# A decoder trunk in fp32: how the first branch's operands get their norm, and how the norm's reciprocal roots are stored

## The chip, the cores and the metric

The kernel runs on 1 core of a Trainium2 chip. The metric is the device time of one execution in microseconds (us). The engines are PE (matrix products and transposes; PEld is its weight load, which overlaps), DVE, ACT and POOL (element work), and SP, which here issues nearly all transfers. Each engine and SP's queue take their instructions strictly in the order in which the program lists them; an instruction that waits holds all behind it on that engine.

## The reference

One layer of a decoder trunk, with x of [1, 1024, 1024] in fp32. One input projection feeds three token mixers; their outputs are gated, summed, projected and added to x; an MLP follows. Branch A, the first, is differential attention with 4 heads of value width 128, and it ends in a norm over each head's 128 values, a gain (`subln`) and the branch's own projection:

```
w   = p[0] - lam * p[1]                      # two softmaxes of one head
o_A = einsum('bhqk,bhke->bqhe', w, v)        # 4 heads x 128 values per token
y_A = o_A * rsqrt(mean(o_A * o_A, -1) + EPS) * subln   (times a constant)
y_B = sliding-window attention (8 heads); y_C = sparse attention (8 heads)
x  <- x + W_o(sum over n of sigmoid(G_n) * (y_n @ P_n))
x  <- x + W_down relu(W_up RMSNorm(x))^2
```

## The kernel before, in words

**Precision.** Each fp32 matrix is split into a rounded part and a remainder, `hi` and `lo`. `split` (L86 to L91) does this with an ACT copy (L90) and a subtraction on DVE or POOL (L91), and `mm3` (L113 to L120) makes one product from three matmuls (L118, L119, L120). `weight` (L93 to L103) loads a weight tile into a box `wr` (L100, queue SP), ACT copies it to `wh` (L90), POOL subtracts to `wl` (L91). There are 4 boxes `wr` in the attention of branch A, 2 in that of branch C.

**Stages.** Projection of head 0 (to about 90 us); compression of keys (to 130); branch A, four heads, each beside the projections of the next head (130 to 446); branch B (to 580); branch C in two groups (580 to 860 and 860 to 1200); merge (to 1300); MLP (to 2058). While attention runs in small steps on PE (scores L714, transposes of probabilities L762, value products L894 and L895), `mix` (L167) fills PE with dense work: projections, later gate products (`gates`), and in the second group of branch C the first branch's own projection, `first_branch` (L1148).

**Order.** PE's order is the program's order, set by `mix` from estimated costs. On the other engines and on SP's queue the framework's scheduler sets the order when the kernel is built; it is fixed thereafter. `step` (L698) runs a list `late` of closures a counted number of steps after they are put there.

**A head's end.** For each block `qb` of 256 queries, `values` stores the raw head output `o` to DRAM (`od`, L867). Three steps later `norms` (L875 to L883) sums its squares on PE (L878), and DVE makes the mean plus EPS times the softmax's denominators (L880) in a small tile `sso` of 128 x 2; POOL raises that to -0.5 (L881); SP stores it to `rd` (L883). The store turns columns into a row, so that it consists of 256 elements of 4 bytes, 1 KB in all; there are 16 such stores, 4 in each head. Around the turn from one head to the next the same queue carries the projection's weights (`wr<-wa`, `wr<-wb`) and, once in each of the first three turns, `spread_bias` (L393 to L398): one DRAM-to-DRAM copy `bd<-bs` of 768 KB, issued behind the last of a group of weight loads.

**The first branch.** `first_branch` works in two halves of 512 tokens. In each it runs gate products, and in the midst of them, at their steps 3, 7, 11 and 15, it calls `operand` (L1120) for the heads 0 to 3: load 128 x 512 of `od` into a box `wr` (L1123), which it shares with the weights; load the reciprocal roots of 256 tokens, repeated over 128 partitions, into a box `y` (L1128), twice; multiply both on DVE (L1130), 128 x 256 each, by `subln` and the roots; then `split` into `xh` (ACT) and `xl` (DVE). Then the branch's 8 products follow. `merge_and_mlp` calls `operand` without roots.

**Boxes.** The boxes `tm` (2 of 128 x 1024 floats) serve `project` (a projection's normed queries and keys, which PE transposes at L561) and, in `first_branch`, the gates `g` that the 8 products use.

Of the kernel before, what the change touches and what calls it, by code (L numbers as in the profile page):

```python
# [11 lines left out]
F32 = mybir.dt.float32  # L12
F32R = mybir.dt.float32r
AF = mybir.ActivationFunctionType
ALU = mybir.AluOpType
AX = mybir.AxisListType

P = 128
# [57 lines left out]
class Kernel:  # L76
# [27 lines left out]
    def parts(self, pool=None, bufs=None, tag="w"):  # L104
        pool = pool or self.wp
        if self.other is not None:
            self.turn += 1
            pool = self.other if self.turn % 2 else pool
        return [pool.tile([P, self.w_n], F32R, name=tag + x, tag=tag + x, bufs=bufs or self.w_bufs) for x in "hl"]
# [225 lines left out]
    def constants(self, tmp):  # L335
        nc, a, c = self.nc, self.a, self.ca
        ld = nc.sync.dma_start

        gains = tmp.tile([P, 8, HD], F32, name="gains")
        ld(gains, a["qk_gain"].broadcast_to([P, 8, HD]))  # L340
        stt = nc.vector.scalar_tensor_tensor
        stt(self.gk[:, 0, :], gains[:, 0, :], -0.125, gains[:, 1, :], op0=ALU.mult, op1=ALU.mult)
        stt(self.gk[:, 1, :], gains[:, 2, :], -0.125, gains[:, 3, :], op0=ALU.mult, op1=ALU.mult)
        stt(self.gk[:, 2, :], gains[:, 4, :], -0.125, gains[:, 5, :], op0=ALU.mult, op1=ALU.mult)
        stt(self.gsw[:, 0, :], gains[:, 4, :], -0.125, gains[:, 6, :], op0=ALU.mult, op1=ALU.mult)
        stt(self.gsw[:, 1, :], gains[:, 4, :], -0.125, gains[:, 7, :], op0=ALU.mult, op1=ALU.mult)

        dl = tmp.tile([P, 4, HD], F32, name="dl")
        ld(dl, a["diff_lambda"].broadcast_to([P, 4, HD]))
        pr = tmp.tile([P, 2, HD], F32, name="pr")  # L350
        nc.vector.tensor_tensor(pr, dl[:, 0:4:2, :], dl[:, 1:4:2, :], op=ALU.mult)
        ls = tmp.tile([P, 4], F32, name="ls")
        nc.vector.tensor_reduce(ls[:, 0:2], pr, axis=AX.X, op=ALU.add)
        nc.scalar.activation(ls[:, 2:4], ls[:, 0:2], AF.Exp)
        self.nlam = c.tile([P, 1], F32, name="nlam")
        stt(self.nlam, ls[:, 3:4], -LAM_INIT, ls[:, 2:3], op0=ALU.add, op1=ALU.subtract)
        self.subln = c.tile([P, 1], F32, name="subln")
        ld(self.subln, a["diff_subln"])
        nc.vector.tensor_scalar(self.subln, self.subln, 1.0 - LAM_INIT, None, op0=ALU.mult)
        self.sink = c.tile([P, 2, 8], F32, name="sink")  # L360
        ld(self.sink[:, 0, :], a["sinks"].broadcast_to([P, 8]))
        nc.vector.tensor_scalar(self.sink[:, 1, :], self.sink[:, 0, :], -1.0, None, op0=ALU.mult)
        self.wmask = c.tile([P, P], F32, name="wmask")
        ld(self.wmask, a["c_wmask"])
        self.cval = c.tile([P, 1], F32, name="cval")
        ld(self.cval, a["c_cval"])
        self.pos = c.tile([P, 2, 16], F32, name="pos")
        ld(self.pos, a["cmp_pos"])
        self.cgate = c.tile([P, NT, 24], F32, name="cgate")

        c.tile([P, 56], F32, name="gap2")
        self.kct = c.tile([P, 2, P], F32R, name="kct")
        self.vct = c.tile([P, 2, P], F32R, name="vct")
        nc.gpsimd.memset(self.vct[64:P].bitcast(F32), 0.0)
# [417 lines left out]
    def items_a(self, h, sta):  # L792
        nc, at = self.nc, self.at
        bias = self.bias[:, h, :]
        for qb in range(4):
            pq = [None, None]
            box = {}
# [48 lines left out]
            rows = []  # L846
            for j in range(2):
                t = 2 * qb + j
# [26 lines left out]
            def norms(box=box, qb=qb):  # L875
                pt = self.tr()
                for j in range(2):
                    nc.tensor.matmul(pt[:, j:j + 1], box["o2"][:, j * P:(j + 1) * P], self.ones, start=True, stop=True)  # L878
                ss = at.tile([P, 2], F32, name="sso", tag="sso", bufs=2)
                nc.vector.scalar_tensor_tensor(ss, pt[:, 0:2], 1.0 / P, box["eps"], op0=ALU.mult, op1=ALU.add)  # L880
                nc.gpsimd.tensor_tensor(ss, ss, self.nhalf[:, 0:2], op=ALU.pow)  # L881
                r = self.rd[h]
                nc.sync.dma_start(bass.AP(tensor=r.tensor, offset=r.offset + qb * 256, ap=[[1, P], [P, 2]]), ss)  # L883

            yield dict(rows=rows, groups=groups, end=[norms])

# [230 lines left out]
                nc.sync.dma_start(self.gd[f, :, hs], o)  # L1117


    def operand(self, src, s, hi, lo, rows=None):  # L1120

        raw = self.wp.tile([P, 512], F32, name="wr", tag="wr", bufs=self.wr_bufs)
        self.nc.sync.dma_start(raw, src[:, s])  # L1123
        if rows is not None:
            for o in (0, 256):
                r = self.sq.tile([P, 256], F32, name="y", tag="y", bufs=2)
                src = bass.AP(tensor=rows.tensor, offset=rows.offset + s.start + o, ap=[[0, P], [1, 256]])
                self.nc.sync.dma_start(r, src)  # L1128
                v = raw[:, o:o + 256]
                self.nc.vector.scalar_tensor_tensor(v, v, self.subln, r, op0=ALU.mult, op1=ALU.mult)  # L1130
        self.split(hi, lo, raw)


    def gate(self, pool, tag, bufs, n, d, s):
        nc = self.nc
        g = pool.tile([P, 512], F32, name="g", tag=tag, bufs=bufs)
        nc.sync.dma_start(g, self.gd[n * KT + d, :, s])
        return g
# [9 lines left out]
    def first_branch(self):  # L1148
        nc = self.nc
        for half, n, m in ((0, GATES[3], GATES[4]), (1, GATES[5], 24 - sum(GATES))):  # L1150
            s = slice(half * 512, half * 512 + 512)
            yield from self.gates(n)
            o = [self.parts(tag="x") for _ in range(4)]
            for k, c in enumerate(self.gates(m)):
                if k % 4 == 3 and k // 4 < 4:
                    self.operand(self.od[k // 4], s, *o[k // 4], self.rd[k // 4])
                yield c
            for d in range(KT):
                w = self.weight(self.a["wbr"][0, d], 512)
                g = self.gate(self.sq, "tm", 2, 0, d, s)  # L1160
                ps = self.branch(0, d, [x[0] for x in o], [x[1] for x in o], w)
                with self.tc.high_priority(offset=self.urgent):
                    nc.vector.scalar_tensor_tensor(g, g, 1.0, ps, op0=ALU.add, op1=ALU.mult)
                nc.sync.dma_start(self.yd[d, :, s], g)
                yield 2.6
# [424 lines left out]
```

## Time and profile before

| | |
|---|---|
| median of 3 runs | 2058.51 us (2051.08 to 2060.27) |
| the profiled execution | 2060.21 us, its span 2058.4 us |
| mean clock granted to PE over the span | 0.971 of full |
| matrix engine's weight loads (PEld) | 1630.0 us busy, 79% of the span |
| queue SP in all (q1) | 213.87 MB, 32.7% of 16 transfer engines |
| stage of branch A, 180 to 446 us | PE idle 34 us of 266 |

How to read the rows that follow. A row of the timeline has the start, the duration, the engine, the line, the operation, output and inputs, and in square brackets the idle time of that engine just before and what released it; SPq is SP's queue, where a duration is that of the issue and not of the transfer. A row of transfers has the count, the size of each, and the median time from issue to landing. A row of windows has the stretch, its length, and for PE, PEld, DVE, ACT and POOL the busy time (with the instructions), then the clock granted to PE (1 is full), the share of time the transfer engines were busy, and GB/s. A row of groups has the count, the busy time and the mean nanoseconds of one, and the idle time before them with what ended it. In a row of waits stand the sum, the times and the longest, in us.

### The profile page before, as it was taken

Reading aid. Unit: us, or ns where it says so; the run is one execution under the profiler, and the core shown is the slowest. Engines: PE = TensorE matmul, PEld = TensorE weight load, DVE = VectorE, ACT = ScalarE, POOL = GpSimd, SP = SyncE. Lnnn points to the kernel's source line nnn. Section 1 sums busy time; section 2 is a strip of 40 time slices with the busy share of each in tenths; the row PEclk is TensorE's granted clock in tenths of the full one; section 3 lists DMA queues with packets and bytes.
Section 4 is the critical chain, followed back from the end, with each engine's and each line's share of the span. In section 5 each row is a group of like instructions: output and inputs, shape, how many; then the busy total and the mean of one; then the engine's idle time right before and its main releaser. Section 6 shows DMA issues by size and latency. Waiting matters only on the chain. (4 is left out here: it accounts for less than half of the span.)

```text
span 2058.4 us, 30688 instructions
## 1 busy us (share of the span) xinstructions
PE 1905.6 (93%) x9838; PEld 1630.0 (79%) x9838; DVE 1417.6 (69%) x3232; ACT 1005.4 (49%) x2546; POOL 951.4 (46%) x1142
## 2 busy tenths in 40 slices
PE   7998988989899999998998888999799998999988
PEld 7888878878688888887887677788688886888876
DVE  6756766778848677647677745747755444889898
ACT  5455545556636555535555533325455544444331
POOL 4455445544362212161221327217554445789783
PEclk9999999999999999999999999999999999999998
DMA  5132022211211111203142546424544446345343
GB/s 217 51 103 55 10 54 53 31 31 37 85 29 60 61 47 56 73 32 110 60 133 86 182 173 201 163 91 156 176 165 163 143 149 245 118 165 163 123 143 113
DMA packets 129214, 221.60 MB, mean 108 GB/s; under 512 B 19028, under 2 KB 42068, under 8 KB 129052
## 3 DMA queue, kind: packets, MB, share of 16 engines
q1 hardware_dynamic: 127468, 213.87, 32.7%
q10 hardware_dynamic: 1584, 5.77, 0.8%
q8 instruction: 78, 1.28, 0.3%
q14 instruction: 84, 0.69, 0.1%
HBM read 158.68 MB, written 64.83 MB: 109 GB/s over the span
## 5 line engine op out<-in xcount | busy, mean ns | idle before, releaser
L91 POOL TENSOR_TENSOR wl<-wr,wh 128x512 fp32r<-128x512 f32 (+3 forms) x246 | 328.5, 1341 | 303.2 <-ACT wh L90 260.0
L90 ACT ACTIVATE wh<-wr 128x512 fp32r<-128x512 f32 (+3 forms) x258 | 150.2, 590 | 210.2 <-PE mm L119 113.7
L714 PE MATMUL sc<-st 128*128 128x256 f32 (+5 forms) x736 | 185.9, 347 | 29.4 <-ACT p L746 29.0
L90 ACT ACTIVATE ph<-tr 128x384 fp32r<-128x384 f32 (+3 forms) x280 | 138.6, 498 | 111.3 <-PE tr L762 88.8
L91 DVE TENSOR_TENSOR pl<-tr,ph 128x384 fp32r<-128x384 f32 (+3 forms) x280 | 155.5, 559 | 48.7 <-ACT ph L90 46.7
L759 POOL MEMSET ph<- 128x128 f32 x152 | 34.6, 227 | 298.3 <-PE ac L894 245.8
L714 PEld LDWEIGHTS sc<-st 128*128 128x128 f32 x736 | 125.0, 196 | 50.8 <-ACT p L746 41.8
L118 PE MATMUL mm<-hh,wh 128*128 128x512 f32 x384 | 161.6, 421 | 0.0
L762 PE MATMUL tr<-ident,p 128*128 128x128 f32 x792 | 132.8, 281 | 27.7 <-DVE st L567 23.6
L119 PE MATMUL mm<-hl,wh 128*128 128x512 f32 x384 | 154.3, 402 | 0.0
L120 PE MATMUL mm<-hh,wl 128*128 128x512 f32 x384 | 153.9, 401 | 0.0
L119 PE MATMUL mm<-wl,wh 128*128 128x512 f32 x352 | 140.5, 399 | 9.5 <-POOL wl L91 9.5
L118 PE MATMUL mm<-wh 128*128 128x512 f32 x352 | 140.4, 399 | 8.3 <-DVE x L1472 5.4
L90 ACT ACTIVATE wh<-u 128x512 fp32r<-128x512 f32 x162 | 93.0, 620 | 108.0 <-PE mm L119 29.4
L120 PE MATMUL mm<-wh,wl 128*128 128x512 f32 x352 | 139.6, 397 | 0.0
L746 ACT ACTIVATE p<-sc,mc 128x256 f32<-128x256 f32 (+5 forms) x200 | 106.8, 539 | 52.7 <-DVE mc L738 48.4
L894 PE MATMUL ac<-ph,st 128*128 128x256 f32 x392 | 111.1, 301 | 19.1 <-DVE ob L901 9.8
L91 POOL TENSOR_TENSOR wl<-s,wh 128x512 fp32r<-128x512 f32 x64 | 89.1, 1400 | 77.8 <-ACT wh L90 77.8
L762 PEld LDWEIGHTS tr<-ident,p 128*128 128x128 f32 x792 | 95.7, 145 | 29.6 <-DVE st L567 24.9
L118 PE MATMUL mm<-wh,hh 128*128 128x384 f32 (+1 forms) x320 | 118.0, 369 | 0.6 <-ACT raw L523 0.6
L91 DVE TENSOR_TENSOR wl<-u,wh 128x512 fp32r<-128x512 f32 x98 | 112.0, 1145 | 4.0 <-ACT wh L90 4.0
L895 PE MATMUL ac<-pl,st 128*128 128x256 f32 x392 | 107.0, 293 | 7.3 <-DVE pl L91 6.7
(307 smaller groups left out, 5744.0 us busy)
## 6 DMA issues: line engine op xcount, KB each, us to landing
ud<-u SPq DMA_DIRECT2D x112, 256.0 KB, 2.1
u<-ud SPq DMA_DIRECT2D x98, 256.0 KB, 3.4
wr<-wu SPq DMA_DIRECT2D x76, 256.0 KB, 2.8
wr<-wd SPq DMA_DIRECT2D x64, 256.0 KB, 3.0
gd<-go SPq DMA_DIRECT2D x48, 256.0 KB, 2.0
g<-gd SPq DMA_DIRECT2D x48, 256.0 KB, 3.1
wr<-wg SPq DMA_DIRECT2D x40, 256.0 KB, 2.8
wr<-wbr SPq DMA_DIRECT2D x40, 256.0 KB, 2.9
```

Of the source, the lines that this page charges most:

```text
L90: nc.scalar.activation(hi, src, AF.Copy)
L91: (eng or nc.vector).tensor_tensor(lo, src, hi.bitcast(F32), op=ALU.subtract)
L118: mm(out, lh, rh, start=first, stop=False, skip_group_check=more)
L119: mm(out, lh, rl, start=False, stop=False, skip_group_check=more)
L120: mm(out, ll, rh, start=False, stop=last, skip_group_check=more)
L714: self.nc.tensor.matmul(ps[:, off:off + k1 - k0], q[:, t * P:(t + 1) * P], k[:, k0:k1], start=i == 0, stop=i == 1)
L746: self.nc.scalar.activation(p, ps, AF.Exp, bias=m, scale=-1.0, accum_out=l)
L759: nc.gpsimd.memset(ph[0:rows, o:o + P].bitcast(F32), 0.0)
L762: nc.tensor.transpose(pt[0:rows, o:o + P], src, self.ident)
L894: nc.tensor.matmul(ac, v, ph, start=first, stop=False)
L895: nc.tensor.matmul(ac, v, pl, start=False, stop=last)
```

## The change

**The roots.** DVE writes the sums of all four blocks of a head into one tile `rms` of 128 x 8 on chip. Only after the fourth does POOL raise all 8 columns to -0.5, in one instruction, and three steps later `rows_of_head` transposes them on PE to 8 x 128, ACT copies them to `rr`, and SP stores them to `rd` as 8 rows of 512 bytes.

**The operands.** `scaled` takes the place of `operand` in `first_branch`. A box `tm` holds 512 columns of the raw head output in its first half and the repeated roots of the same 512 tokens in its second (two loads). When the step comes, POOL multiplies the one by the other, ACT makes `xh` with `subln` as its scale, DVE makes `xl` in one instruction. The loads for heads 0 and 1 are listed ahead of the gate products, those of heads 2 and 3 once the parts of heads 0 and 1 are listed. These operands no longer use boxes `wr` or `y`.

```diff
-        c.tile([P, 56], F32, name="gap2")
+        self.rms = c.tile([P, 4, 8], F32, name="rms")
+        c.tile([P, 24], F32, name="gap2")
...
-                ss = at.tile([P, 2], F32, name="sso", tag="sso", bufs=2)
+                ss = self.rms[:, h, 2 * qb:2 * qb + 2]
                 nc.vector.scalar_tensor_tensor(ss, pt[:, 0:2], 1.0 / P, box["eps"], op0=ALU.mult, op1=ALU.add)
-                nc.gpsimd.tensor_tensor(ss, ss, self.nhalf[:, 0:2], op=ALU.pow)
-                r = self.rd[h]
-                nc.sync.dma_start(bass.AP(tensor=r.tensor, offset=r.offset + qb * 256, ap=[[1, P], [P, 2]]), ss)
+                if qb == 3:
+                    r = self.rms[:, h, :]
+                    nc.gpsimd.tensor_tensor(r, r, self.nhalf, op=ALU.pow)
+                    self.late.append([3, rows_of_head])
+
+            def rows_of_head():
+                pt = self.tr()
+                nc.tensor.transpose(pt[0:8, 0:P], self.rms[:, h, :], self.ident)
+                r = at.tile([8, P], F32, name="rr", tag="sso", bufs=1)
+                nc.scalar.activation(r, pt[0:8, 0:P], AF.Copy)
+                nc.sync.dma_start(self.rd[h].rearrange("(t j) -> t j", j=P), r)
...
+    def scaled(self, i, s, hi, lo):
+        nc = self.nc
+        box = self.sq.tile([P, self.tm_n], F32, name="tm", tag="tm", bufs=2)
+        raw, r = box[:, 0:512], box[:, 512:1024]
+        row = self.rd[i]
+        nc.sync.dma_start(raw, self.od[i, :, s])
+        nc.sync.dma_start(r, bass.AP(tensor=row.tensor, offset=row.offset + s.start, ap=[[0, P], [1, 512]]))
+
+        def parts():
+            nc.gpsimd.tensor_tensor(raw, raw, r, op=ALU.mult)
+            nc.scalar.activation(hi, raw, AF.Copy, scale=self.subln)
+            nc.vector.scalar_tensor_tensor(lo, raw, self.subln, hi.bitcast(F32), op0=ALU.mult, op1=ALU.subtract)
+
+        return parts
...
+            parts = [self.scaled(i, s, *o[i]) for i in range(2)]
             for k, c in enumerate(self.gates(m)):
-                if k % 4 == 3 and k // 4 < 4:
-                    self.operand(self.od[k // 4], s, *o[k // 4], self.rd[k // 4])
+                if k % 4 == 3 and parts:
+                    parts.pop(0)()
+                    if k < 8:
+                        parts.append(self.scaled(2 + k // 4, s, *o[2 + k // 4]))
                 yield c
```

**Order on SP's queue, second head turn.** Before, the weight loads of the next projection (`wr<-wa`, `wr<-wb`) and the roots' stores (`rd<-sso`) stand so:

```order
L867 DMA od<-o_3041 128x256
L100 DMA wr<-wa 128x384
L883 DMA rd<-sso 128x2x1
L100 DMA wr<-wa 128x384 x3
L398 DMA bd_782<-bs 128x4x384
L100 DMA wr<-wb 128x396 x3
```

Now, with `rd<-rr` for the 8 rows of a head:

```order
L868 DMA od<-o_3031 128x256
L100 DMA wr<-wa 128x384 x4
L399 DMA bd_783<-bs 128x4x384
L100 DMA wr<-wb 128x396 x4
L868 DMA od<-o_3245 128x256
L892 DMA rd<-rr 8x128
```

The store from between the weight loads is gone; the head's one store stands behind all of them. The other turns change alike; at the third turn one `wr<-wb` stands right behind an `rd<-rr`.

**Order on SP's queue, first half of the first branch.** Before, where the operands' loads (`wr<-od`, `y<-rd`) follow four gate weights:

```order
L100 DMA wr<-wg 128x512 x4
L1123 DMA wr<-od 128x512
L1128 DMA y<-rd 128x256 x2
L1123 DMA wr<-od 128x512
L1117 DMA gd<-go 128x512
L1128 DMA y<-rd 128x256 x2
```

Now, at the same place:

```order
L100 DMA wr<-wg 128x512 x6
L1126 DMA gd<-go 128x512
L100 DMA wr<-wg 128x512
L1141 DMA tm<-od 128x512
L1142 DMA tm<-rd 128x512
L1126 DMA gd<-go 128x512
L100 DMA wr<-wg 128x512
L1141 DMA tm<-od 128x512
```

The gate weights come ahead of the operands' loads. The box of the first waits for the last projection's use of it; the third and fourth wait for the parts of heads 0 and 1.

**Order on ACT, second half of the first branch.** Before, the four `xh` copies stand among the exponentials (`p`, `pc`) and the copies of transposed probabilities (`ph`):

```order
L1116 ACTIVATE go<-mm 128x512
L90 ACTIVATE xh<-wr 128x512
L746 ACTIVATE pc_7154,lc<-sc,mc 128x64
L90 ACTIVATE ph<-tr 128x384
L90 ACTIVATE xh<-wr 128x512
L746 ACTIVATE p,lc<-sc,mc 128x448
```

Now they stand some 20 rows earlier in the order and are released by POOL's product:

```order
L747 ACTIVATE pc_7131,lc<-sc,mc 128x64
L1146 ACTIVATE xh<-tm,subln 128x512
L90 ACTIVATE ph<-tr 128x512
L747 ACTIVATE p,lc<-sc,mc 128x256
L90 ACTIVATE ph<-tr 128x384
L747 ACTIVATE p,lc<-sc,mc 128x256
```

A copy that waits still holds the exponentials behind it; what it waits for is another engine and other loads.

## The prediction and its working, on record before the run

> **What bounds the kernel now.** The page first. PE is busy nearly all the time, so what can be won is time in which PE waits or is slow.
>
> ```profile
> span 2058.4 us, 30688 instructions
> PE 1905.6 (93%) x9838; PEld 1630.0 (79%) x9838; DVE 1417.6 (69%) x3232; ACT 1005.4 (49%) x2546; POOL 951.4 (46%) x1142
> ```
>
> The change touches two places, branch A (the roots' stores) and the first branch inside branch C (the operands). For branch A, the waits of PE from 150 to 450 us, then PE's own rows after its four longest waits:
>
> ```profile
> PE tr L762 <- DVE st L567: 23.6, 7, 6.8
> ...
> 198.97 1.12 PE L762 MATMUL tr<-ident,p 128*128 128x128 f32 x4 [3.89 <-DVE pl L91]
> ...
> 270.02 1.11 PE L762 MATMUL tr<-ident,p 128*128 128x128 f32 x4 [6.74 <-DVE st L567]
> ...
> 342.58 1.11 PE L762 MATMUL tr<-ident,p 128*128 128x128 f32 x4 [6.81 <-DVE st L567]
> ...
> 415.00 1.12 PE L762 MATMUL tr<-ident,p 128*128 128x128 f32 x4 [6.24 <-DVE st L567]
> ```
>
> These four, one at each head's turn, are 3.89 + 6.74 + 6.81 + 6.24 = 23.7 us. The windows of 4 us behind each show the granted clock (the number before the last two):
>
> ```profile
> 199.00:203.00 4.00, 4.00 (x15) 4.00 (x16) 3.31 (x13) 2.78 (x9) 1.44 (x2) 0.50 0.73 227
> 270.00:274.00 4.00, 3.98 (x21) 3.96 (x22) 2.86 (x9) 1.81 (x6) 2.93 (x4) 0.64 0.39 126
> 342.50:346.50 4.00, 3.92 (x17) 3.92 (x18) 3.66 (x10) 1.06 (x4) 3.40 (x4) 0.50 0.15 50
> 415.00:419.00 4.00, 4.00 (x17) 3.90 (x17) 2.78 (x11) 0.80 (x2) 2.15 (x3) 0.50 0.30 82
> ```
>
> At a clock c, 4 us do the work of 4c, so each loses 4 x (1 - c): 2.0 + 1.4 + 2.0 + 2.0 = 7.4 us more. Whence the wait? DVE had waited for ACT, and ACT for a weight. At the second turn, ACT's row and the queue's issues, and, from the transfers' rows for these two issues, what each took to land:
>
> ```profile
> 266.11 0.52 ACT L90 ACTIVATE wh<-wr 128x384 fp32r<-128x384 f32 x1 [6.87 <-DMA wr<-wa]
> ...
> 256.61 0.37 SPq L883 DMA_DIRECT2D rd<-sso  x1
> 257.60 3.97 SPq L100 DMA_DIRECT2D wr<-wa  x3
> ...
> rd<-sso SPq DMA_DIRECT2D x1, 1.0 KB, 8.0
> ...
> wr<-wa SPq DMA_DIRECT2D x1, 192.0 KB, 8.5
> ```
>
> The weight issued at 257.60 landed 8.5 us later, at 266.1, where ACT resumes. The store ahead of it carries 1 KB and takes 8.0 us. The third turn has the counter-check within a microsecond, a weight issued just ahead of a store and three just behind it:
>
> ```profile
> 328.33 0.33 SPq L100 DMA_DIRECT2D wr<-wb  x1
> 328.99 0.37 SPq L883 DMA_DIRECT2D rd<-sso  x1
> 330.01 4.27 SPq L100 DMA_DIRECT2D wr<-wb  x3
> ...
> wr<-wb SPq DMA_DIRECT2D x1, 198.0 KB, 2.4
> ...
> wr<-wb SPq DMA_DIRECT2D x3, 198.0 KB, 9.1
> ```
>
> 2.4 us ahead of it, 9.1 behind. The other suspect is the copy `bd<-bs` of 768 KB near by. At the fourth turn none is in the queue, and still a weight behind a store takes 7.0 us; from 117 to 136 us, twelve weights with such a copy among them land in 2.9:
>
> ```profile
> 401.13 0.37 SPq L883 DMA_DIRECT2D rd<-sso  x1
> 403.71 2.62 SPq L100 DMA_DIRECT2D wr<-wb  x3
> ...
> wr<-wb SPq DMA_DIRECT2D x1, 198.0 KB, 7.0
> ...
> wr<-wa SPq DMA_DIRECT2D x12, 192.0 KB, 2.9
> bd<-bs SPq DMA_DIRECT2D x1, 768.0 KB, 7.0
> ```
>
> For the first branch, the groups from 900 to 1110 us (DVE's product with the roots, ACT's copy of an operand), PE's rows after its long waits, and the windows behind those:
>
> ```profile
> L1130 DVE SCALAR_TENSOR_TENSOR wr<-wr,subln,y 128x256 f32<-128x256 f32 x16 | 8.0, 508 | 6.3 <-DMA y<-rd 6.3
> ...
> L90 ACT ACTIVATE xh<-wr 128x512 fp32r<-128x512 f32 x8 | 5.0, 629 | 10.5 <-DVE wr L1130 10.5
> ...
> 934.48 0.76 PE L714 MATMUL sc<-st 128*128 128x512 f32 x2 [1.94 <-ACT p L746]
> ...
> 948.11 0.50 PE L714 MATMUL sc<-st 128*128 128x256 f32 x2 [2.15 <-ACT p L746]
> ...
> 1094.41 0.80 PE L714 MATMUL sc<-st 128*128 128x256 f32 x2 [4.62 <-ACT p L746]
> ...
> 934.40:938.40 4.00, 3.92 (x12) 3.07 (x13) 3.94 (x14) 2.15 (x9) 0.00 (x0) 0.58 0.54 138
> 948.10:952.10 4.00, 3.99 (x13) 3.17 (x14) 2.95 (x11) 1.61 (x7) 0.23 (x1) 0.57 0.51 156
> 1094.40:1098.40 4.00, 3.99 (x10) 3.24 (x11) 2.17 (x6) 2.11 (x7) 0.00 (x0) 0.50 0.46 134
> ```
>
> ACT waits for DVE, DVE for the roots; the exponentials stand behind ACT's copy and PE behind those. First half: 1.94 + 2.15 idle, 1.7 + 1.7 slow, 7.5 us in all. Second half: 4.62 + 2.0 = 6.6. Together 14.1 us.
>
> **The change part by part.** *Sixteen stores become four.* At each turn the store between the weights is gone, and by the 2.4 us above the weights then land in time. What could return is 23.7 + 7.4 = 31.1 us. Against it stands that one weight still follows a store of the new form, at the third turn. No row shows a store of 8 rows: its bounds are 0 us of stall, and one whole stall with its slow clock, 6.81 + 2.0 = 8.8. I take 4, about the middle, since the store of 256 elements is the one row for `rd` but this one has 8 pieces. Gain 27.1, bounds 22.3 and 31.1.
>
> *The transposes.* Four more on PE's path, at the 0.29 of the row below: 1.1 us. Each waits for POOL's power, issued three steps earlier. Four copies on ACT, at most 0.52 each as in ACT's row above, stand ahead of copies that PE waits for: 0 to 2.1 us; I take 0, as they are beside an ACT that would otherwise still wait. Sixteen powers of 0.71 us become four of 0.71 to 2.85 (four times the columns, if time goes by columns): POOL has 0 to 8.5 us less to do, off the path; I count 0.
>
> ```profile
> L881 POOL TENSOR_TENSOR sso<-sso,nhalf 128x2 f32<-128x2 f32 x16 | 11.4, 712 | 6.7 <-DVE sso L880 6.2 <-DVE lb L931 0.6
> ...
> 952.28 0.29 PE L561 MATMUL tr<-identr,tm 128*128 128x128 f32 x2
> ```
>
> *The operands' loads.* In the second half the boxes lie idle before: both loads of heads 0 and 1 can be in place long before the step, and the 6.6 us go. In the first half the last projection still reads its box at 952.28, which is later than both stalls, and the loads of heads 2 and 3 wait in turn for the first two; what I take away there I give back: 0 of 7.5. Bounds for both: 0 and 14.1. Gain 6.6.
>
> *The products.* POOL takes 8 products, DVE drops 16 of 0.508. The nearest row for the product is POOL's subtraction of the same shape, 1.34 us, so 10.7 in all; POOL was idle in two of the three stalls' windows above (0.00 busy), which hides it, and where that cover is gone, 1.34 is added to a copy that PE waits for, 10.7 at most. DVE may lose by a neighbour: of the old subtractions `xl`, one took 0.68 and one, at 947.5, 1.34, beside a POOL operation:
>
> ```profile
> L91 POOL TENSOR_TENSOR wl<-wr,wh 128x512 fp32r<-128x512 f32 x25 | 33.5, 1338 | 66.7 <-ACT wh L90 64.0 <-DVE lc L1037 2.7
> ...
> L91 DVE TENSOR_TENSOR xl<-wr,xh x2: 683/1011/1339, 942.1 to 947.5; 128x512 fp32r<-128x512 f32 x2
> ...
> 947.06 1.26 POOL L91 TENSOR_TENSOR wl<-wr,wh 128x512 fp32r<-128x512 f32 x1 [5.62 <-ACT wh L90]
> ```
>
> So each new product may cost DVE 0.66: 5.3, less than the 8.0 it drops. I count 0. The Trainium skill's page "SBUF — State Buffer", section "SBUF: two separate sides", speaks against this move: a VectorE operation with two inputs on chip and a GpSimd operation that reads there shut each other out for a whole instruction. The row at 947.5 agrees. By that rule DVE could lose up to a whole product each time, and with POOL's 1.34 the estimate is 10.7 against 8.0: 2.7 us more on DVE in place of 2.7 less.
>
> *Slow clock.* I count 1.7 us after waits of 1.94 and 2.15 us because the windows show 0.58 and 0.57 there. The Trainium skill's page "TensorE: Matmul & The Clock Gate", section "Part 1: The HAM clock gate", says that the clock drops only after an idle window of about 3.4 us. The rows here differ: it was low after shorter waits. By the rule the two short waits have no slow clock to give back, and the most for the first branch would be 10.7 instead of 14.1.
>
> *Sum.* 27.1 + 6.6 - 1.1 = 32.6 us off. From the profiled execution's 2060.2 that is 2027.6. The median of the runs stands 1.7 lower, at 2058.5; from it, 2025.9, so **2026**. All at their best, 31.1 + 14.1 - 1.1 = 44.1, give 2014; all at their worst, 22.3 + 0 - 1.1 - 2.1 = 19.1, give 2039.
>
> **The rivals.** *The big copy is what delays the weights.* It is still in three of the turns, right behind the first weights. Then only the fourth turn is won, 6.24 + 2.0 = 8.2, and the sum is 8.2 + 6.6 - 1.1 = 13.7: **2044.8**. For it: `bd<-bs` takes 7.0 us, much as the late weights. Against: the fourth turn, and the twelve weights at 2.9.
>
> *Two boxes are too few.* Heads 2 and 3 can be loaded only after heads 0 and 1 are done; four loads in the two halves then cost PE a whole landing, with 2 us of slow clock each.
>
> ```profile
> wr<-od SPq DMA_DIRECT2D x24, 256.0 KB, 3.9
> ```
>
> 4 x (3.9 + 2.0) = 23.6 in place of 14.1, 9.5 lost: 27.1 - 9.5 - 1.1 = 16.5 off, **2042**. For it: the order, where these loads wait. Against: a gate's steps lie between.
>
> *Slower: the operands stall the softmax every time.* ACT's `xh` now waits for POOL, which waits for two loads; POOL's queue (weights' `wl`, clearing of `ph` and `pl`) and ACT's exponentials stand behind. If all 8 operands cost a landing and slow clock, 8 x 5.9 = 47.2 are lost, against 27.1 - 1.1 = 26.0 won: 21.2 slower, **2080**. It decides from 26.0 / 8 = 3.3 us per operand on, and can be measured from (26.0 + 10.3) / 8 = 4.5. Against: the old operands had the same two kinds of loads and stalled PE at length in three places.
>
> *The store is no quicker.* If 8 rows land as late as 256 elements and the head's one store delays weights at each turn, branch A gains nothing: 6.6 - 1.1 = 5.5 off, **2053**. Against: the order puts the store behind the weights.
>
> **How the numbers follow.** Forecast 0.70, big copy 0.12, two boxes 0.09, slower 0.05, store no quicker 0.04. A measurement of this kernel can tell about 0.5% from no change, 10.3 us, so faster means below 2048.2. Faster: forecast, two boxes and two thirds of the big copy's chance (its 2044.8 lies near the bound), 0.87; same: the other third and the slow store, 0.08; slower 0.05. The forecast and two boxes alone hold 0.79, so the range goes on to the big copy's time: 2014 to 2046.
>
> **What would show it.** Right: at the four turns no wait of PE over 2 us, weights landing in 2.4 to 2.9, clock near 1 behind; four stores `rd<-rr`; no stall near the second half's operands. Big copy: the first three turns still stall and the fourth doesn't. Two boxes: POOL's product waits for `tm<-od`, and PE for exponentials behind it. Wrong altogether if the weights land in 2.9 us at the turns and PE still waits there, for DVE itself or for another engine.

## The result, and the profile after

| | before | changed |
|---|---|---|
| median of the runs | 2059.16 us (2051.08 to 2060.27, 4 runs) | 2024.68 us (2018.51 to 2025.22, 4 runs) |
| ratio | | 0.9834, 95% interval 0.9802 to 0.9866 |
| span of the profiled execution | 2058.4 us | 2022.4 us |
| mean clock granted to PE | 0.971 | 0.982 |

The changed kernel is 34.5 us faster; the forecast was 2026 us, 32.6 us off. The sum came out; one of its terms did not, and a gain for which it had no term took that place, as the stages show. The page of the changed kernel: PE's busy time fell by 16 us, so a part of the gain is not idle time but faster matmuls.

```profile
PE 1889.4 (93%) x9842; PEld 1618.3 (80%) x9842; DVE 1410.4 (70%) x3216; ACT 1006.0 (50%) x2550; POOL 953.8 (47%) x1138
```

The waits of PE from 150 to 450 us in the changed kernel, the row that was 23.6 us:

```profile
PE tr L763 <- DVE st L568: 8.3, 7, 1.9
```

PE's own rows at the four turns of the changed kernel:

```profile
193.69 0.55 PE L763 MATMUL tr<-ident,p 128*128 128x128 f32 x3 [1.22 <-DVE st L568]
...
259.06 0.44 PE L763 MATMUL tr<-ident,p 128*128 128x128 f32 x2 [1.01 <-DVE st L568]
...
325.32 0.48 PE L763 MATMUL tr<-ident,p 128*128 128x128 f32 x1 [1.93 <-DVE st L568]
...
392.61 0.66 PE L763 MATMUL tr<-ident,p 128*128 128x128 f32 x4 [1.77 <-DVE st L568]
```

The waits are 1.0 to 1.9 us where they were 3.9 to 6.8. The weights of the second turn (first four, and second four right behind the copy of 768 KB) and of the fourth turn, where no copy stands, with the time to landing last:

```profile
wr<-wa SPq DMA_DIRECT2D x4, 192.0 KB, 2.8
...
wr<-wb SPq DMA_DIRECT2D x4, 198.0 KB, 7.0
...
wr<-wb SPq DMA_DIRECT2D x4, 198.0 KB, 2.6
```

So the weights right behind the big copy are late (3.3 us with the copy elsewhere, in the run with copies and boxes moved below), but they are not the ones that PE waits for.

Three instructions stand in every kernel's order on PE, and between them lie two stages: from a score product near 135 us to a value product near 730 us (most of branch A, branch B, the first part of branch C; stage 1), and on to the last transpose of branch C near 1160 us (stage 2, with the first branch). Before:

```profile
134.92:759.13 624.21, 563.56 (x3372) 509.69 (x3372) 449.06 (x1411) 348.54 (x1096) 259.88 (x487) 0.96 0.19 45
759.13:1195.39 436.26, 404.20 (x2253) 345.56 (x2254) 305.65 (x937) 238.55 (x668) 119.32 (x209) 0.98 0.28 88
```

The changed kernel:

```profile
136.62:729.00 592.38, 550.73 (x3375) 498.92 (x3375) 448.18 (x1411) 349.02 (x1100) 254.97 (x475) 0.99 0.16 47
729.00:1160.28 431.28, 401.48 (x2253) 344.10 (x2254) 298.78 (x921) 238.62 (x668) 128.92 (x217) 0.99 0.28 89
```

Stage 1 is 31.8 us shorter. Its idle time of PE went from 624.21 - 563.56 = 60.7 to 592.38 - 550.73 = 41.7, 19.0 less; the other 12.8 us are the same matmuls in less time. Stage 2 is 5.0 us shorter in this profile.

### The profile page after: what moved, and what is told of

It reads as the page before. It is cut to its first block, busy times and chain, and to the rows that moved or that the text cites. A ratio compares the mean times of both kernels' runs of the same rounds, so it can differ in the third digit from the quotient of the medians.

```text
span 2022.4 us, 30612 instructions
## 1 busy us (share of the span) xinstructions
PE 1889.4 (93%) x9842; PEld 1618.3 (80%) x9842; DVE 1410.4 (70%) x3216; ACT 1006.0 (50%) x2550; POOL 953.8 (47%) x1138
## 5 line engine op out<-in xcount | busy, mean ns | idle before, releaser
L119 PE MATMUL mm<-wl,hh 128*128 128x384 f32 (+1 forms) x320 | 109.7, 343 | 0.0
```

The costliest lines, as they stand in the source:

```text
L119: mm(out, lh, rl, start=False, stop=False, skip_group_check=more)
```

## The experiments

Twelve runs followed. They ask, in this order, which part of the change carries the gain, what at the turns delayed the weights and how, and what the operands are worth.

### One part at a time

The roots alone: `rows_of_head` and the tile `rms` as changed, `operand` and its call as before.

> The changed kernel with the old operands in the first branch; only the roots are handled in the new way. Theory (small stores hold up the weights at the head turns): the gain of branch A stays whole, the long waits of PE at the four turns are all under 2 us, about 30 us off: 2029, between 2026 and 2034. Rival (the gain needs the new operands too, since the old ones give it back in the first branch): 2045 or more.

Measured: 2024.32 us, ratio to before 0.9840 (0.9808 to 0.9871). Its two stages:

```profile
135.16:725.61 590.45, 551.46 (x3375) 498.70 (x3375) 449.35 (x1411) 349.13 (x1100) 255.24 (x475) 0.99 0.16 47
725.61:1162.88 437.27, 406.12 (x2253) 347.33 (x2253) 306.22 (x937) 237.93 (x668) 120.41 (x209) 0.98 0.29 88
```

The roots alone are as fast as the whole change. The operands alone, `scaled` with the stores of before:

> The kernel before with the new operands only; the roots are stored as 16 x 256 elements as before. Theory: the four turns stall as before (3.9, 6.7, 6.8, 6.2 us), the first half of the first branch gains nothing, the second half 3 to 5: 2054, between 2052 and 2057. Rival (two boxes are too few): 2060 or more. Rival (most of the gain comes from the operands): below 2045.

Measured: 2059.57 us, ratio 1.0006 (0.9988 to 1.0024). That is above what the theory allowed (2057) and just short of the rival's 2060: no gain that can be measured.

```profile
134.57:756.55 621.98, 561.30 (x3372) 507.47 (x3372) 448.37 (x1411) 348.12 (x1096) 259.41 (x487) 0.96 0.19 45
756.55:1192.99 436.44, 404.96 (x2253) 346.17 (x2253) 301.78 (x921) 238.73 (x668) 129.00 (x217) 0.98 0.28 88
```

### The stores put back, twice

The first try stored the sums from the tile `rms` itself:

```diff
+                x = self.rx[h]
+                nc.sync.dma_start(bass.AP(tensor=x.tensor, offset=x.offset + qb * 256, ap=[[1, P], [P, 2]]), ss)
                 if qb == 3:
                     r = self.rms[:, h, :]
```

> The changed kernel with 16 more stores of 256 elements of 4 bytes, at the end of each block as before, into a scratch row that nobody reads (they carry the sums before the power). POOL's powers, the transposes and the new operands stay as changed. Theory (the store itself delays the weights behind it): stalls of 4 to 7 us are back at the turns where the store stands ahead of or among the weights, 20 to 30 us slower than the changed kernel: 2045 to 2055. Rival (the powers on POOL, or the order of the scheduler, made the difference): within 4 us of 2025.

Measured: 2084.95 us, ratio 1.0125 (1.0099 to 1.0152), slower than either theory said. POOL's waits from 150 to 470 us name a second cause that the edit brought in: the power works in place on the tile that the store still reads.

```profile
POOL rms L887 <- DMA rx<-rms: 13.0, 2, 7.3
```

The scheduler also put the stores elsewhere in SP's queue. So this run says that the stores cost, but not how much. The second try gives the store its own tile and its own power, as before:

```diff
+                y = at.tile([P, 2], F32, name="ssx", tag="ssx", bufs=2)
+                nc.gpsimd.tensor_tensor(y, ss, self.nhalf[:, 0:2], op=ALU.pow)
+                x = self.rx[h]
+                nc.sync.dma_start(bass.AP(tensor=x.tensor, offset=x.offset + qb * 256, ap=[[1, P], [P, 2]]), y)
                 if qb == 3:
```

> The changed kernel with the 16 powers of 128 x 2 and the 16 stores of 256 elements put back beside the new way, from a small tile of their own into a scratch row that nobody reads. They stand in SP's queue where they stood before the change, and no later instruction on the way to the result waits for their landing. Theory (the store alone costs the gain): the four turns stall again, 3 to 7 us each, 2053 to 2062. Rival (the excess of the first such run, 2085, was the stores themselves and not the power waiting for them): 2075 or more. Rival (the new operands or the batching carry the gain): 2025 to 2030.

Measured: 2061.76 us, ratio 1.0016 (0.9994 to 1.0037). The whole gain is gone, and PE's rows at the second, third and fourth turn stand as they stood before the change:

```profile
268.67 0.69 PE L764 MATMUL tr<-ident,p 128*128 128x128 f32 x2 [5.96 <-DVE st L569]
...
341.79 1.11 PE L764 MATMUL tr<-ident,p 128*128 128x128 f32 x4 [6.67 <-DVE st L569]
...
414.44 0.90 PE L764 MATMUL tr<-ident,p 128*128 128x128 f32 x3 [6.57 <-DVE st L569]
```

Nobody reads what these stores write. With their powers on POOL (0.7 us each in the kernel before), they are all that this kernel has over the changed one.

### The big copy

The kernel before, with all five copies during the compression:

```diff
-            self.spread_bias(0)
+            for i in range(5):
+                self.spread_bias(i)
...
-            self.spreads.append(h + 1)
```

> The kernel before with all five copies of 768 KB issued during the compression (about 115 us) instead of one at each head turn; the stores of 256 elements stay. Theory (the small store delays the weights): the four turns stall as before, 2055 to 2063. Rival (the big copy delays them): the first three turns no longer stall, the fourth does as before, about 24 us off: 2035.

Measured: 2057.49 us, ratio 0.9995 (0.9977 to 1.0012). With no copy at any turn, the second and the third stall as before, and the fourth still waits 4.05 us:

```profile
266.96 0.48 PE L762 MATMUL tr<-ident,p 128*128 128x128 f32 x1 [6.88 <-DVE st L567]
...
339.75 0.47 PE L762 MATMUL tr<-ident,p 128*128 128x128 f32 x1 [7.09 <-DVE st L567]
...
412.36 0.48 PE L762 MATMUL tr<-ident,p 128*128 128x128 f32 x1 [4.05 <-DVE st L567]
```

The rival of the big copy falls.

### How a store of 1 KB delays a weight

The prediction spoke of the weight behind the store in the queue. Is it the queue? The kernel before, with the store issued by ACT:

```diff
-                nc.sync.dma_start(bass.AP(tensor=r.tensor, offset=r.offset + qb * 256, ap=[[1, P], [P, 2]]), ss)
+                nc.scalar.dma_start(bass.AP(tensor=r.tensor, offset=r.offset + qb * 256, ap=[[1, P], [P, 2]]), ss)
```

> The kernel before with one edit: the 16 stores are issued from ACT's queue instead of SP's, same shape, same count. Theory (what waits is what stands behind the store in the same queue): weights land in 2.4 to 3, the four turns are free, minus what ACT pays for 16 issues and for waiting on POOL's power: 2026 to 2038. Rival (256 small pieces hold the transfer engines themselves, whatever the queue): weights still land in 7 to 9, 2052 or more.

Measured: 2057.96 us, ratio 0.9987 (0.9975 to 0.9998): the theory of the queue falls. The second turn, ACT's issue and its wait, and the transfers of that turn:

```profile
257.79 0.37 ACTq L883 DMA_DIRECT2D rd<-sso  x1
267.49 0.52 ACT L90 ACTIVATE wh<-wr 128x384 fp32r<-128x384 f32 x1 [7.28 <-DMA wr<-wa]
...
wr<-wa SPq DMA_DIRECT2D x4, 192.0 KB, 8.8
rd<-sso ACTq DMA_DIRECT2D x1, 1.0 KB, 7.5
```

No store is in SP's queue, and the weights that SP issues about it still land in 8.8 us. ACT resumes on its weight 2.2 us after the store's landing (257.79 + 7.5 = 265.3). The run settles another rival too, that the weights are late because they are issued late. In the kernel before, SP's queue stands still for the powers on POOL that the stores wait for, 12 times and 63.9 us in all from 180 to 446 us. With the stores on ACT's queue this wait is gone from SP's, and nothing is won.

What the two queues share is the transfer engines. Their share of time and GB/s (the last two numbers) while the weight is late, and in the changed kernel at the same turn, with the big copy among the weights:

```profile
259.50:267.40 7.90, 4.82 (x34) 4.38 (x32) 1.85 (x5) 0.71 (x2) 4.05 (x4) 0.94 0.79 39
...
256.50:264.50 8.00, 6.99 (x55) 6.85 (x54) 6.90 (x23) 5.86 (x22) 6.40 (x9) 1.00 0.84 232
```

The engines are busy for about the same share of the time, and move 39 GB/s where they move 232 without the small store. The Trainium skill's page "DMA: Bandwidth & Descriptors", section "Queues, rings and completion order", says that the queues of SP and ACT each have a ring on the same 16 transfer engines, and that an engine's completion signal lands only after all its earlier writes, whatever queue they came from. The run agrees in that the weight lands behind the store, from either queue. But at 39 GB/s the weights' data itself is held up, not only the signal of its end, so the rule on signals is not shown to be the cause; what makes the engines slow stays open.

Next the form of the store, first alone: 128 pieces of 8 bytes instead of 256 of 4, with SP's order the same row by row (the roots land permuted, so the first branch multiplies by other tokens' roots).

```diff
-ap=[[1, P], [P, 2]]), ss)
+ap=[[2, P], [1, 2]]), ss)
```

> The kernel before with one edit: each of the 16 stores writes 128 pieces of 8 bytes instead of 256 of 4 (the roots land in another order in DRAM, so the first branch multiplies by the wrong tokens' roots). The order on SP is the same row by row. Theory (the landing goes by the number of pieces): it halves, 8.0 to about 4, weights behind it land in 4.5 to 5.5, the stalls at the turns shrink by some 3 to 4 us each and their slow clock mostly stays: 2038 to 2050. Rival (the cost is that of any tiny store, not of the count): the stalls stay, 2055 to 2062.

Measured: 2033.89 us, ratio 0.9884 (0.9861 to 0.9906), better than the theory's bound. The store's row from 180 to 446 us, 8.1 in the kernel before, and PE at the second to fourth turn:

```profile
rd<-sso SPq DMA_DIRECT2D x16, 1.0 KB, 3.1
...
259.93 0.47 PE L762 MATMUL tr<-ident,p 128*128 128x128 f32 x1 [2.95 <-DVE st L567]
...
330.97 0.47 PE L762 MATMUL tr<-ident,p 128*128 128x128 f32 x1 [3.93 <-DVE st L567]
...
399.16 0.47 PE L762 MATMUL tr<-ident,p 128*128 128x128 f32 x1 [2.88 <-DVE st L567]
```

Then the batch without the transposes: one store of 1024 elements for each head.

```diff
-                pt = self.tr()
-                nc.tensor.transpose(pt[0:8, 0:P], self.rms[:, h, :], self.ident)
-                r = at.tile([8, P], F32, name="rr", tag="sso", bufs=1)
-                nc.scalar.activation(r, pt[0:8, 0:P], AF.Copy)
-                nc.sync.dma_start(self.rd[h].rearrange("(t j) -> t j", j=P), r)
+                r = self.rd[h]
+                nc.sync.dma_start(bass.AP(tensor=r.tensor, offset=r.offset, ap=[[1, P], [P, 8]]), self.rms[:, h, :])
```

> The changed kernel without the transposes: the 8 columns of a head go to DRAM in one store of 1024 elements of 4 bytes, 4 such stores in all, a good part of a head's time ahead of the weights. Theory (landing goes by the number of pieces, 8.0 us for 256): one store takes about 32 us; what is issued behind it within that time is late, the head's own output first, and the weights of the turn where less than that lies between: 2030 to 2050, with stalls at some turns. Rival (it is enough that there are fewer stores and none between the weights): within 4 us of the changed kernel's 2025.

Measured: 2032.39 us, ratio 0.9870 (0.9854 to 0.9887). The time is in the theory's range, but its 32 us are wrong. The store's row, and SP's issues about the third turn:

```profile
rd<-rms SPq DMA_DIRECT2D x4, 4.0 KB, 11.6
...
305.75 0.37 SPq L889 DMA_DIRECT2D rd<-rms  x1
...
315.79 1.33 SPq L100 DMA_DIRECT2D wr<-wb  x2
```

Four times the pieces took 11.6 us, not 32, and the weights of that turn come 10 us behind, where they no longer meet it. So most of the gain, about 27 of 34 us, comes without transposes. Its second stage was 441.0 us, 9.7 longer than in the changed kernel's first profile; the next run bears on that.

### What the operands are worth

> The changed kernel once more, nothing edited, to see how far one profile of it stands for its runs. Branch C's second stage, from the value product at 729.00 to the last transpose at 1160.28, was 431.3 us in its first profile, 436.3 to 437.3 in the four kernels with the old operands, 436.4 to 441.0 in three others with the new ones. Theory now (the operands gain nothing that is certain): this stage comes out at 434 to 440 this time, or the total stays at 2024 with another stage longer. Rival (the 5 us are the new operands' gain): 431 to 432 again.

Measured: 2024.83 us, ratio 0.9846 (0.9822 to 0.9869).

```profile
133.88:723.30 589.42, 547.88 (x3375) 495.89 (x3375) 448.78 (x1411) 348.92 (x1100) 255.00 (x475) 1.00 0.16 47
723.30:1159.79 436.49, 404.97 (x2253) 346.06 (x2254) 302.29 (x921) 238.59 (x668) 129.47 (x217) 0.98 0.28 88
```

The same program, the same time, and now stage 2 has its old length and stage 1 is 34.8 us shorter than before. A gain of 5 us read from one profile of stage 2 was no gain of the operands; with the new operands this stage has been 431.3, 436.5, 436.4 and 441.0 us, with the old ones 436.3 and 437.3. With the product on DVE (below) it was 431.8. Stage 1 keeps its gain in the changed kernel's two profiles and in that of the roots alone: 31.8, 34.8 and 33.8.

Where a gain would have to come from, the first half shows in the changed kernel's first profile: PE's last transposes out of the projection's box, SP's load of the third operand that waited for them, POOL's product that waits for that load, and PE behind ACT.

```profile
917.08 0.29 PE L562 MATMUL tr<-identr,tm 128*128 128x128 f32 x2
...
917.40 0.32 SPq L1141 DMA_DIRECT2D tm<-od  x1
...
922.51 1.26 POOL L1145 TENSOR_TENSOR tm<-tm 128x512 f32<-128x512 f32 x1 [3.02 <-DMA tm<-rd]
...
926.59 0.58 PE L715 MATMUL sc<-st 128*128 128x256 f32 x1 [3.77 <-ACT p L747]
```

To take that wait away, four boxes of the operands' own:

```diff
-        box = self.sq.tile([P, self.tm_n], F32, name="tm", tag="tm", bufs=2)
+        box = self.sq.tile([P, 1024], F32, name="tq", tag="tq", bufs=4)
```

> The changed kernel with four boxes of the operands' own (128 x 1024 each) in place of the two shared with the projections: the scheduler issues the first half's eight loads hundreds of us ahead, and the second half's in the first half. No operand's product can wait for its load or for a box. Theory (what the new operands gain is given back to the wait for boxes in the first half: 3.8 us of PE and about 2 us of slow clock at 926.6): 2016 to 2022. Rival (the waits of PE for exponentials come from DVE and ACT being late anyway): 2023 to 2028.

Measured: 2021.96 us (2018.69 to 2026.57), ratio 0.9833 (0.9808 to 0.9858), beside 2024.83 for the changed kernel on the same chip. The value is the theory's, but the intervals overlap. Stage 2:

```profile
725.73:1151.95 426.22, 399.58 (x2252) 341.42 (x2252) 303.40 (x921) 236.56 (x664) 118.83 (x209) 1.00 0.26 83
```

It is 10.3 us shorter than in the changed kernel beside it. But from its end to the last instruction it is 2018.8 - 1151.95 = 866.9 us here and 2020.4 - 1159.79 = 860.6 there: 6.3 of the 10.3 us are given back later. Most of that is one wait in the merge: PE waits 5.7 us there for the products with the gates on DVE (`g`, L1218), 4.5 us in the run that follows, and next to nothing (0.1 us) with two boxes.

With the copies moved into the compression as well (the edit shown above):

> The four boxes, and all five copies of 768 KB issued during the compression instead of one at each of the turns. In the changed kernel the second four weights of the turns, right behind the copy, land in 4.8, 7.0 and 6.6 us against 2.4 to 2.8 of the first four. Theory (PE does not wait for those second four): within 3 us of the run with four boxes alone. Rival (with the small stores gone the copy is what is late next): 4 to 8 us faster than that run.

Measured: 2019.13 us (2015.91 to 2021.49), ratio 0.9817 (0.9792 to 0.9841). It is 2.8 us below the run with four boxes, within what the theory allowed. All its four runs lie below all four of the changed kernel on the same chip (2022.21 to 2027.52), and it has the lowest median of all the kernels; the two ratios' intervals still overlap.

The last one changes the product's engine:

```diff
-            nc.gpsimd.tensor_tensor(raw, raw, r, op=ALU.mult)
+            nc.vector.tensor_tensor(raw, raw, r, op=ALU.mult)
```

> The changed kernel with the eight products on DVE instead of POOL; nothing else is edited. Theory (the product's engine is hidden either way): within 4 us of the changed kernel. Rival (POOL's products hold DVE up where both read two inputs on chip, up to 0.66 us each, 5 us): 4 or more faster. Rival (DVE is what the exponentials' inputs wait for, so 8 more operations of about 0.7 on it show): 5 or more slower.

Measured: 2024.55 us, ratio 0.9851 (0.9823 to 0.9879): no difference. The groups of `xl` and of the product on DVE, from 880 to 1110 us:

```profile
L1147 DVE SCALAR_TENSOR_TENSOR xl<-tm,subln,xh 128x512 fp32r<-128x512 f32 x8 | 7.1, 884 | 0.0
...
L1145 DVE TENSOR_TENSOR tm<-tm 128x512 f32<-128x512 f32 x8 | 6.1, 764 | 5.5 <-DMA tm<-rd 5.5
```

The product is quicker here, 0.76 against POOL's 1.30, and it makes no odds. `xl` has no POOL product beside it now and takes 0.88; with the products on POOL it took 0.85. The fear that POOL's products hold DVE up found nothing here.

## Why the prediction was right, and where it was not

**The stores at the turns: right.** The stores alone carry the gain (put back, 2061.8 us), and the big copy does not (moved, 2057.5 us). The order of SP's queue was read rightly as to what meets what, but a weight is not late because it stands behind the store in that queue: issued from ACT's queue, the store costs the same. What counts is that store and weight are under way at the same time.

**The size of branch A's term: right, and a gain in branch B that has no term.** 27.1 - 1.1 = 26.0 us were forecast for branch A. Stage 1 gave 31.8, 33.8 and 34.8, but it ends far behind branch A. The same value product, near the end of branch A in every kernel, cuts the stage in two; before, in the changed kernel's first profile, and in its second:

```profile
134.92:440.48 305.56, 270.37 (x1684) 255.45 (x1684) 218.32 (x652) 167.19 (x531) 146.80 (x229) 0.94 0.21 39
440.48:759.13 318.65, 293.19 (x1688) 254.23 (x1688) 230.73 (x760) 181.35 (x567) 113.08 (x258) 0.97 0.17 50
...
136.62:416.87 280.25, 264.72 (x1687) 250.67 (x1687) 218.36 (x652) 167.63 (x534) 141.25 (x217) 0.98 0.15 42
416.87:729.00 312.13, 286.00 (x1688) 248.25 (x1688) 229.82 (x760) 181.39 (x568) 113.72 (x258) 1.00 0.17 52
...
133.88:411.43 277.55, 262.07 (x1687) 247.84 (x1688) 218.90 (x652) 167.53 (x534) 141.11 (x217) 0.99 0.15 43
411.43:723.30 311.87, 285.81 (x1688) 248.05 (x1688) 229.88 (x760) 181.39 (x568) 113.88 (x258) 1.00 0.17 52
```

Branch A is 25.3 and 28.0 us shorter. PE's idle time there fell from 35.2 to 15.5 us both times; these 19.7 are the 23.7 less the 4 held back. PE's busy time fell by 5.7 and 8.3 us, where 7.4 were put for the slow clock. The 4 came out by luck: they were meant for one late weight at the third turn, but what is left stands at all four, 1.22 + 1.01 + 1.93 + 1.77 = 5.9 us.

The other 6.5 and 6.8 us come behind branch A, where the change edits nothing until the second group of branch C and the prediction counted nothing. PE's idle time is no smaller there (25.5 us before, 26.1 in both profiles after), its busy time is 7.2 and 7.4 us smaller, and the clock is 1.00 instead of 0.97. Before, the slow clock follows waits in branch B, and most of them are still there: the same value product waits 1.97 us at 493.50 before and 1.96 at 466.13 in the changed kernel, and the 4 us behind it have a clock of 0.65 and of 1.00. So this part is not the price of a stall at a turn. The last section shows what decides between the two; with the roots alone it was 4.7 us.

**The transposes, copies and powers: as counted.** The four powers took 1.64 us each, inside the bounds of 0.71 and 2.85; the 1.1 us of transposes is too small to be seen beside the rest.

**The operands' term: wrong.** 6.6 us were forecast, from the second half's stall of 4.62 us and its slow clock; alone the operands gave nothing (1.0006, 0.9988 to 1.0024), and beside the new store nothing either (2024.3 without them, 2024.7 and 2024.8 with them). The stall of 4.62 did go, but other waits stand in its place: in the second profile of the changed kernel PE waits 2.42 us for exponentials at 1039.55, and from the value product at 974.32 the rest of stage 2 lasts 185.5 us, where from the same product at 1011.30 it lasted 184.1 before. That the first half would give back what it won was right: the third load waited for the projection's box.

**The sum.** Branch A gave 25.3 to 28.0 for the 26.0 of the sum, the operands nothing for their 6.6, and branch B 6.5 to 6.8 from outside the sum, so that 32.6 met a measured 34.5. The forecast was right by its main mechanism, and as close as it was by luck.

**The rivals.** The big copy is refuted by the run without it at the turns (2057.5 us). The prediction's argument from twelve weights at 2.9 us did not show it: the profile gives no landing for the two issued right behind the copy there, so the median leaves them out. Refuted are also the store that is no quicker (no turn stalls over 2 us) and the slower softmax (stage 2 is no longer than before by more than its profiles differ). Two boxes are too few in the sense that four made stage 2 shorter in both of their profiles (426.2 and 427.8 us), but the two lost nothing against before.

## What to carry to other kernels

Judge a store by its pieces, not by its bytes: 1 KB in 256 pieces of 4 bytes kept weights of 200 KB waiting for 6 us, and another queue doesn't help; fewer, longer pieces or another moment do. Set a forecast's term against the stretch of which it speaks, cut at fixed instructions: over all of stage 1 branch A's term looked 6 to 9 us too small, over branch A it was right within 2 us, and the rest was slow clock elsewhere. And a stage's gain of 1% seen in one profile needs a second profile of the same program before it is put down to an edit.

## What the runs showed of the hardware

**Pieces.** Median landings: 256 pieces of 4 bytes 8.1 us, 128 of 8 bytes 3.1, 1024 of 4 bytes 11.6. That is in proportion neither to the pieces nor to the bytes; what sets it stays open. The pieces themselves pass quickly: in the kernel before, 287 transfers under 512 bytes stand between 257.5 and 258.5 us, and the store lands at 256.61 + 8.0 = 264.6. The profile gives no landing for the 8 rows of 512 bytes.

**The clock.** In the changed kernel's first profile the windows of 4 us behind the first three turns had these clocks:

```profile
193.70:197.70 4.00, 4.00 (x30) 3.88 (x31) 3.39 (x10) 1.95 (x6) 2.22 (x3) 1.00 0.99 215
259.00:263.00 4.00, 3.94 (x30) 3.89 (x31) 2.95 (x11) 2.84 (x10) 3.43 (x4) 1.00 0.86 225
325.30:329.30 4.00, 3.98 (x21) 3.96 (x21) 2.84 (x8) 1.28 (x5) 2.39 (x3) 0.58 0.78 215
```

At the fourth turn PE waits 1.77 us in this profile and 1.73 in the second one of the same program. The clock is low behind the first wait and not behind the other, so a wait's length alone doesn't decide. What does can be read from the clock's own record: in all 14 traces its changes lie on a grid of 3.41 us, which stands differently to the program in each execution. In such steps, the fourth turn in the first profile (two rows) and in the second (three):

```profile
390.09:393.50 3.41, 1.64 (x15) 1.56 (x14) 2.88 (x10) 1.78 (x8) 2.82 (x4) 1.00 0.47 143
393.50:396.91 3.41, 3.41 (x14) 3.30 (x13) 1.79 (x7) 1.23 (x4) 1.17 (x1) 0.50 0.17 60
...
384.44:387.86 3.42, 2.51 (x20) 2.38 (x19) 2.81 (x5) 2.28 (x9) 3.42 (x6) 1.00 0.60 177
387.86:391.27 3.41, 2.59 (x18) 2.55 (x19) 3.38 (x13) 1.01 (x3) 2.29 (x3) 1.00 0.31 101
391.27:394.68 3.41, 3.41 (x28) 3.38 (x27) 2.06 (x11) 3.09 (x13) 1.00 (x2) 1.00 0.07 24
```

Where the whole wait falls into one step, PE is busy for 1.64 of 3.41 us and the next step has half the clock. Where the wait lies across two steps, PE is busy for 2.51 and 2.59 us and the clock stays. Counted over the 14 traces from 130 us on, no step at full clock in which PE was idle for less than 1.3 us was followed by a slow one, and each with 2.0 us or more was; in between both occur. It is the same with the wait of branch B: 1.44 us busy in the step around it before, 2.40 and 2.47 in the two steps after. So the place on the grid where a wait of about 2 us falls is worth up to 1.7 us by estimate (half of a step at half the clock), and it can differ from one execution of a program to the next.

The Trainium skill's page "TensorE: Matmul & The Clock Gate", section "Part 1: The HAM clock gate", says that the activity window runs freely, without regard to the program, which fits the grid and the two answers to the same wait; its 3.4 us of idleness before the clock falls do not fit a low clock after 1.77 us.
